# One fused transformer kernel on one core: the preparation of a state-space layer is spread over GpSimd and more buffers

## The chip, the cores and the metric

The kernel runs on 1 core of one Trainium2 chip. The metric is the device time of one execution in microseconds (us); the kernel before takes 1915.66 us, the median of 3 runs.

## The reference

The reference is two transformer blocks one after the other on 512 tokens of width 1024, in float32. The first has three branches (a chunked state-space scan, a gated linear recurrence and attention to a memory of 256 rows) that are gated, added and projected. The second has four layers, of which the first, a diagonal complex state-space layer called S5, matters here. Cut to its core:

```python
dt = jnp.exp(log_dt)[:, None]
ab = jnp.exp(lam * dt)                      # complex, (groups, states)
bb = (ab - 1) / lam * b                     # complex, (groups, states, 16)
bu = einsum('blgh,gph->blgp', u, bb)
s  = linear recurrence s_t = ab * s_(t-1) + bu_t
y  = gelu(real(einsum('blgp,ghp->blgh', s, c)) + d_skip * u)
out = (y * sigmoid(y @ w_glu + b_glu) * silu(z)) @ w_out
```

The memory attention, whose steps share the preparation's stretch of time, is softmax(q k^T / 16) v with 4 heads of 256 columns and 256 memory rows.

## The kernel before, in words

All wide matrix products are made of three float32r products each (high and low halves), so that TensorE is busy nearly all the time. A weight tile of 128x1024 is loaded by SP into one of 3 buffers, ScalarE rounds it to its high half (L317) and VectorE makes the low half (L318), into one of 7 pairs of buffers. Working tiles of 128x512 come from a pool of 36 (class Slots); it is a first-in, first-out list, and what is given back is handed out again in that order. A tile framework tracks the dependences, puts the instructions of each engine in an order before the run, by priority and a model of their durations, and adds the waits. SP issues the transfers in one queue; ScalarE and GpSimd have queues of their own.

**The preparation** (`s5_prep`, L1285) turns the parameters of S5 into tables in device memory: for each of 8 blocks b of 4 group pairs an input table W (winD), a response table E (eD) and a Toeplitz table T (toD). It has nothing to do with the tokens, and it is woven, by `yield`, into the last part of the linear recurrence and into the memory attention (`mem_`, L1152: 1.3 steps of the preparation for each step of the attention). Per block: L1380 to L1401 load the parameters and make bbr, bbi on VectorE; L1405 to L1413 make E with six VectorE operations (all through `tt`, L1288) and store it; L1418 to L1432 multiply on TensorE, put the result in Z, which is the first 256 columns of the buffer W0, and store it eight times, shifted, as T; L1434 to L1445 make W: for r = 0, 1 three VectorE operations of 128x512 write the factor into the one buffer f, four transposes (L1443) read it, ScalarE copies the result into W0 (L1444), and W0 is stored.

During one attention head (`mem_core`, L1092) the pool of 36 is held thus: 8 for `merged`, 4 keys, 4 values, 12 of the preparation (a8s, ps_, sc, PT 2, E0 2, W0 2, t, f, RT), prm and bbt, and the head's 2 queries: 32. Each of the four softmax rows of 128 tokens takes one buffer e from those left (L1116), and gives it back after its transposes (L1119) are issued.

**S5 itself** (`s5`, L1450): for each block m `inputs` multiplies u, sends it through device memory (uD, stored by ScalarE's queue at L1475, loaded by GpSimd's at L1478) to change its layout, and loads W. `starts` (L1486) makes chunk states, `scan` (L1500) runs the recurrence on VectorE in two halves, `within` (L1572) applies T, `outputs` (L1584) applies E to the states: ScalarE copies states (L1590), TensorE multiplies, VectorE adds (L1596), ScalarE applies gelu (L1598) and stores (L1599), GpSimd's queue loads the result in the other layout (L1602). `parts` (L1606) then splits y in halves for the next product (`split`: ScalarE at L471, VectorE at L472). `advance`, inside `scan`, takes two adjacent buffers for its products anew in each of its four calls. The loads of E (`fetch_e`, L1557) and T (`fetch_t`, L1545) go through SP's queue; E of blocks 0 to 3 goes to buffers that are free early.

Of the kernel before, what the change touches and what calls it, by code (L numbers as in the profile page):

```python
# [11 lines left out]
F32 = mybir.dt.float32  # L12
F32R = mybir.dt.float32r
I32 = mybir.dt.int32
AF = mybir.ActivationFunctionType
ALU = mybir.AluOpType
AX = mybir.AxisListType
PSUM = bass.MemoryType.PSUM
P = 128
# [188 lines left out]
class Kern:  # L208
# [258 lines left out]
    def split(self, hi, lo, src, scale=None):  # L467

        nc = self.nc
        if scale is None:  # L470
            nc.scalar.copy(hi, src)  # L471
            nc.vector.tensor_tensor(out=lo, in0=src, in1=hi.bitcast(F32), op=ALU.subtract)  # L472
        else:
            nc.scalar.activation(hi, src, AF.Copy if isinstance(scale, float) else AF.Identity, scale=scale)  # L474
            nc.vector.scalar_tensor_tensor(out=lo, in0=src, scalar=scale, in1=hi.bitcast(F32),  # L475
                                           op0=ALU.mult, op1=ALU.subtract)

    def wide(self):

# [805 lines left out]
    def s5_prep(self):  # L1285
        nc, S, I, p = self.nc, self.S, self.i, self.p
        V = nc.vector
        tt = lambda o, a, b, op: V.tensor_tensor(out=o, in0=a, in1=b, op=op)  # L1288
# [5 lines left out]
        ps_ = S.get()  # L1294
# [7 lines left out]
        sc = S.get()  # L1302
        w = [sc[:, 32 * j:32 * j + 32] for j in range(16)]
        PT, pts = S.run(2)
        PT = PT.rearrange("p a b -> p (a b)")[:, :576].rearrange("p (r j q) -> p r j q", r=2, j=9)
        E0, es = S.run(2)
        W0, ws = S.run(2)
        t, f = S.get(), S.get()
        RT = S.get()
        RT_ = RT.rearrange("p (r j q) -> p r j q", r=2, j=8)  # L1310
        dt, mag, th = w[0], w[1], w[2]
        self.exp_acc(dt, ld, w[8:12])
# [67 lines left out]
        for b in range(8):  # L1380
            qs = slice(4 * b, 4 * b + 4)
            prm = S.get()
            self.dma(out=prm[:, :256], in_=I["s5bc"][b])
            br, bi, cr, ci = [q4(prm[:, 64 * j:64 * j + 64]) for j in range(4)]
            nci = q4(prm[:, 256:320])
            V.tensor_scalar(nci, ci, -1.0, None, op0=ALU.mult)
            bbt = S.get()
            bbr, bbi, t1 = [q4(bbt[:, 64 * j:64 * j + 64]) for j in range(3)]
            f4 = lambda f: f[:, qs].unsqueeze(2).to_broadcast([P, 4, 16])
            tt(bbr, br, f4(fr), ALU.mult)  # L1390
            tt(t1, bi, f4(fi), ALU.mult)
            tt(bbr, bbr, t1, ALU.subtract)
            tt(bbi, bi, f4(fr), ALU.mult)
            tt(t1, br, f4(fi), ALU.mult)
            tt(bbi, bbi, t1, ALU.add)

            bd = bbt[:, 256:512].rearrange("p (r q z h) -> p r q z h", r=2, q=4, z=2)
            V.memset(bbt[:, 256:512], 0.0)
            for r, s in ((0, bbr), (1, bbi)):
                for z in range(2):  # L1400
                    V.tensor_copy(bd[64 * z:64 * z + 64, r, :, z], s[64 * z:64 * z + 64])  # L1401
            yield
            pw = lambda T, r, a: T[:, r, a:a + 8, qs].rearrange("p j q -> p q j").unsqueeze(3).to_broadcast([P, 4, 8, 16])
            x8 = lambda x: x.unsqueeze(2).to_broadcast([P, 4, 8, 16])
            E = E0.rearrange("p a b -> p (a b)").rearrange("p (q r n) -> p q r n", q=4, r=2)  # L1405
            ev = lambda r: E[:, :, r].rearrange("p q (j h) -> p q j h", j=8)
            tt(ev(0), pw(PT, 0, 1), x8(cr), ALU.mult)
            tt(q8(t), pw(PT, 1, 1), x8(ci), ALU.mult)
            tt(ev(0), ev(0), q8(t), ALU.subtract)
            tt(ev(1), pw(PT, 0, 1), x8(nci), ALU.mult)  # L1410
            tt(q8(t), pw(PT, 1, 1), x8(cr), ALU.mult)
            tt(ev(1), ev(1), q8(t), ALU.subtract)
            self.dma(out=self.eD[b], in_=E.rearrange("p q r n -> p (q r n)"))  # L1413
            yield

            g = self.tb()[:, 0:P]
            bl = lambda r, q: bd[:, r, q].rearrange("p z h -> p (z h)")
            self.in_order(True)  # L1418
            for r, c in ((0, cr), (1, nci)):
                for q in range(4):  # L1420
                    self.mm(g[32 * q:32 * q + 32, 0:16], bl(r, q), c[:, q], r == 0, r == 1)
            for r in range(2):
                for q in range(4):
                    self.mm(g[32 * q:32 * q + 32, 16:128], bl(r, q), E[:, q, r, 0:112], r == 0, r == 1)
            self.in_order(False)
            Z = W0.rearrange("p a b -> p (a b)")[:, 0:256]
            V.memset(Z[:, 0:128], 0.0)
            V.scalar_tensor_tensor(out=g[:, 0:16], in0=eye, scalar=dsk[:, b:b + 1], in1=g[:, 0:16], op0=ALU.mult, op1=ALU.add)
            nc.scalar.copy(Z[:, 128:256], g)
            dst = self.toD[b].rearrange("(t r q n) -> t q r n", t=8, r=32, q=4)  # L1430
            for k in range(8):
                self.dma(out=dst[k], in_=Z[:, 128 - 16 * k:256 - 16 * k])  # L1432
            yield
            W = W0.rearrange("p a b -> p (a b)").rearrange("p (q r n) -> p q r n", q=4, r=2)  # L1434
            for r in range(2):
                u, v, op = ((bbr, bbi, ALU.subtract), (bbi, bbr, ALU.add))[r]
                tt(q8(f), pw(RT_, 0, 0), x8(u), ALU.mult)
                tt(q8(t), pw(RT_, 1, 0), x8(v), ALU.mult)
                tt(f, f, t, op)
                yield  # L1440
                o = self.tb().rearrange("p (q n) -> p q n", q=4)
                for q in range(4):
                    nc.tensor.transpose(o[:, q], f[:, q * P:(q + 1) * P], self.ident)  # L1443
                nc.scalar.copy(W[:, :, r], o)  # L1444
            self.dma(out=self.winD[b], in_=W.rearrange("p q r n -> p (q r n)"))  # L1445
            S.put(prm, bbt)
            yield
        S.put(ps_, sc, RT, t, f, *pts, *es, *ws)

    def s5(self):  # L1450
        nc, S, R, I = self.nc, self.S, self.R, self.i
# [6 lines left out]
        SA, sas = S.run(8)  # L1458
# [27 lines left out]
        def starts(ms):  # L1486

            for m in ms:
                W, ws = Ws[m]
                v = self.tb().rearrange("p (r q c) -> p r q c", r=2, q=4)  # L1490
                for q in range(4):
                    for r in range(2):
                        for z in range(2):
                            self.mm(v[64 * z:64 * z + 64, r, q], W[:, q, r, 64 * z:64 * z + 64], g8(us[m])[:, 2 * q + z],
                                    True, True)
                nc.scalar.copy(SA[:, :, 4 * m:4 * m + 4, 1:64], v[:, :, :, 0:63])
                S.put(*ws)
                yield

        def scan(n):  # L1500
# [2 lines left out]
            qs = slice(16 * n, 16 * n + 16)  # L1503
            X = SA[:, :, qs]
            V = nc.vector
            prs = S.get()
            pr = [prs[:, 64 * j:64 * j + 64].rearrange("p (c r q) -> p c r q", c=2, r=2) for j in range(2)]

            def advance(k, src, dst, m):

                tmp, ts_ = S.run(2)
                t = tmp.rearrange("p a b -> p (a b)")[:, :32 * m].rearrange("p (r q c) -> p r q c", r=2, q=16)
                for c in range(2):
                    V.tensor_tensor(out=t, in0=X[:, :, :, src], op=ALU.mult,
                                    in1=self.a8[:, k, c, :, qs].unsqueeze(3).to_broadcast([P, 2, 16, m]))
                    V.tensor_tensor(out=t[:, 0], in0=t[:, 0], in1=t[:, 1], op=ALU.add)

                    V.tensor_tensor(out=X[:, c, :, dst], in0=X[:, c, :, dst], in1=t[:, 0], op=ALU.add)
                    yield
                S.put(*ts_)  # L1520

            yield from advance(0, slice(0, 63, 2), slice(1, 64, 2), 32)
            yield from advance(1, slice(1, 62, 4), slice(3, 64, 4), 16)
# [7 lines left out]
            S.put(prs)  # L1531
            yield from advance(1, slice(3, 60, 4), slice(5, 62, 4), 15)
            yield from advance(0, slice(1, 62, 2), slice(2, 63, 2), 31)

        zs, ys = [], []
        yh, yl = [R.get(), R.get()], [R.get(), R.get()]

        def gates(n):
# [18 lines left out]
        def fetch_e(m):  # L1557


            r, a = (yh, yl)[m // 2 % 2][m < 4], 2 * (m % 2)  # L1560
            Es[m] = [r[:, a + j].bitcast(F32) for j in range(2)]
            for j in range(2):
                last.append(self.dma(out=Es[m][j], in_=self.eD[m][:, 512 * j:512 * j + 512]))

        def fetch(f, *ms):

# [17 lines left out]
        def outputs(ms):  # L1584
            for m in ms:
# [6 lines left out]
                for q in range(4):  # L1592
                    for r in range(2):
                        self.mm(o[:, q * P:(q + 1) * P], E[q // 2][:, q % 2, r], B[:, r, q].rearrange("p z c -> p (z c)"),
                                r == 0, r == 1)
                nc.vector.tensor_tensor(out=us[m], in0=us[m], in1=o, op=ALU.add)  # L1596
                t = S.get()
                nc.scalar.activation(t, us[m], AF.Gelu_apprx_tanh)  # L1598
                nc.scalar.dma_start(out=by_time(yD[m]), in_=t)  # L1599
                S.put(t, us[m])  # L1600
                y = S.get()
# [3 lines left out]

        def parts(ms):  # L1606
            for m in ms:
                self.split(yh[m // 4][:, m % 4], yl[m // 4][:, m % 4], ys[m])
            yield

        run(inputs(range(5), self.gemm_early(True)))
# [539 lines left out]
```

## Time and profile before

| | |
|---|---|
| median of 3 runs | 1915.66 us (1913.89 to 1918.42) |
| the profiled execution, its own time | 1913.85 us |
| its span, first to last instruction | 1911.8 us |
| granted TensorE clock, mean | 0.994 of full speed |
| TensorE busy | 1866.1 us, 98% of the span |
| VectorE busy | 1298.0 us, 68% |
| ScalarE busy | 893.4 us, 47% |
| GpSimd busy | 57.3 us, 3% |

The profile is that of one execution. An engine's busy time is the sum of the time in which it ran an instruction; the time before an instruction in which its engine stood idle is put down to what released it. TensorE's ends are modelled, so that its busy share says that work was queued, not that the array was full. The preparation runs from about 665 to 950 us of the span, S5 from about 1000 to 1140 us.

### The profile page before, as it was taken

The page shows a single profiled execution, that of the slowest core. Times are in us where ns is not written, and L with a number is a line of the kernel's source. Part 1 is how long each engine was busy: PE and PEld are TensorE (multiplying, and loading weights), DVE is VectorE, ACT ScalarE, POOL GpSimd, SP SyncE. Part 2 cuts the span into 40 slices and gives each one's busy share as a digit, 9 for nine tenths or more (in the row PEclk, how much of TensorE's full clock was granted, in tenths as well). Part 3 has the DMA queues.
Part 4 walks back from the last instruction along what each step waited for, and adds up shares of the span by engine and source line. Part 5 has one row for each costly group of instructions (what it writes and reads, how often), then busy time and mean ns, then how long its engine had stood idle before and what let it go on. Part 6 is the DMA issues. An engine that isn't in the chain of part 4 may idle for free. (4 is left out here: it accounts for less than half of the span.)

```text
span 1911.8 us, 26275 instructions
## 1 busy us (share of the span) xinstructions
PE 1866.1 (98%) x9843; PEld 1517.1 (79%) x9843; DVE 1298.0 (68%) x2579; ACT 893.4 (47%) x1666; POOL 57.3 (3%) x93
## 2 busy tenths in 40 slices
PE   8999999999999999999999999999999999999998
PEld 7788877888888788778778878888887677788887
DVE  7886777665467897675475955787664776758553
ACT  5655545363565644332343444465544555534231
POOL 0100000000000000000001010000000000000000
PEclk9999999999999999999999999999999999999999
DMA  5543323323233436434668544232323122333421
GB/s 184 152 138 111 105 85 105 120 67 113 82 114 100 124 121 227 137 116 127 198 219 276 183 143 130 70 116 78 101 100 99 53 64 67 99 122 110 133 77 44
DMA packets 99201, 229.90 MB, mean 120 GB/s; under 512 B 18081, under 2 KB 38977, under 8 KB 99074
## 3 DMA queue, kind: packets, MB, share of 16 engines
q1 hardware_dynamic: 86192, 216.85, 35.3%
q0 software_dynamic: 2544, 6.00, 1.2%
q10 hardware_dynamic: 10338, 5.38, 1.0%
q8 instruction: 77, 1.26, 0.3%
q14 instruction: 50, 0.41, 0.1%
HBM read 200.28 MB, written 26.35 MB: 119 GB/s over the span
## 5 line engine op out<-in xcount | busy, mean ns | idle before, releaser
L277 PE MATMUL g<-rt,wh 128*128 128x512 f32 (+1 forms) x3664 | 1100.9, 383 | 11.2 <-ACT rt L471 7.4
L277 PEld LDWEIGHTS g<-rt,wh 128*128 128x128 f32 x3664 | 671.4, 190 | 147.5 <-ACT rt L471 9.1
L277 PE MATMUL g<-rt,wl 128*128 128x512 f32 (+1 forms) x1816 | 682.6, 380 | 0.0
L317 ACT CAST wh<-wf 128x1024 fp32r<-128x1024 f32 (+2 forms) x300 | 300.8, 1011 | 466.7 <-PE g L277 343.4
L318 DVE TENSOR_TENSOR wl<-wf,wh 128x1024 fp32r<-128x1024 f32 (+2 forms) x300 | 350.2, 1174 | 246.0 <-ACT wh L317 234.0
L277 PEld LDWEIGHTS g<-rt,wl 128*128 128x128 f32 x1816 | 343.8, 189 | 62.7 <-issue 1.9
L277 PE MATMUL g<-wh,rt 128*128 128x512 f32 x992 | 310.6, 393 | 0.7 <-DVE rt L475 0.7
L277 PEld LDWEIGHTS g<-wh,rt 128*128 128x128 f32 x992 | 185.6, 189 | 40.3 <-DVE rt L475 1.0
L277 PE MATMUL g<-wl,rt 128*128 128x512 f32 x496 | 194.0, 391 | 0.0
L277 PEld LDWEIGHTS g<-wl,rt 128*128 128x128 f32 x496 | 93.5, 189 | 19.7 <-issue 0.3
L277 PE MATMUL t<-st 128*64 128x64 f32 (+8 forms) x746 | 76.6, 274 | 5.7 <-DMA st<-uD 2.0
L665 DVE SCALAR_TENSOR_TENSOR st<-g,pc,st 128x511 f32<-128x511 f32 (+2 forms) x108 | 79.8, 744 | 2.0 <-ACT st L662 1.3
L1288 DVE TENSOR_TENSOR st<-st 128x512 f32<-128x512 f32 (+4 forms) x180 | 76.5, 467 | 6.3 <-PE t L1443 5.1
L275 PE MATMUL t<-st 128*64 128x128 f32 (+4 forms) x788 | 72.1, 296 | 0.8 <-ACT st L708 0.8
L277 PEld LDWEIGHTS t<-st 128*64 128x64 f32 (+3 forms) x746 | 44.1, 141 | 30.2 <-issue 16.4
L275 PEld LDWEIGHTS t<-st 128*64 128x64 f32 (+1 forms) x788 | 54.1, 143 | 16.2 <-issue 10.5
L1224 DVE TENSOR_TENSOR st<-g,st 128x512 f32<-128x512 f32 x32 | 22.0, 689 | 61.2 <-ACT st L1223 61.2
L277 PE MATMUL g<-st 128*128 128x256 f32 (+2 forms) x192 | 56.5, 426 | 5.6 <-DVE st L1265 2.4
L474 ACT ACTIVATE rt<-st 128x512 fp32r<-128x512 f32 x52 | 35.5, 711 | 50.4 <-DVE st L1649 16.3
L1223 ACT ACTIVATE st<-g 128x512 f32<-128x512 f32 x32 | 19.1, 597 | 77.5 <-PE g L277 77.5
L769 ACT ACTIVATE st<-st 128x128 f32<-128x128 f32 x128 | 40.7, 392 | 24.0 <-POOL st L765 23.8
L475 DVE SCALAR_TENSOR_TENSOR rt<-st,rt 128x512 fp32r<-128x512 f32 x52 | 38.4, 760 | 18.1 <-ACT rt L474 16.2
(303 smaller groups left out, 1838.7 us busy)
## 6 DMA issues: line engine op xcount, KB each, us to landing
wf<-in_w_xbc SPq DMA_DIRECT2D x24, 512.0 KB
wf<-in_w_gt SPq DMA_DIRECT2D x24, 512.0 KB
wf<-in_w_z SPq DMA_DIRECT2D x16, 512.0 KB
wf<-in_w_bs SPq DMA_DIRECT2D x16, 512.0 KB
rt<-acsD SPq DMA_DIRECT2D x24, 256.0 KB
wf<-in_w_lx SPq DMA_DIRECT2D x12, 512.0 KB
wf<-in_w_lg SPq DMA_DIRECT2D x12, 512.0 KB
wf<-in_w_bl SPq DMA_DIRECT2D x16, 384.0 KB
```

What stands on the lines that cost most here:

```text
L275: r = self.nc.tensor.matmul(out=out, lhsT=lhsT, rhs=rhs, start=start, stop=stop)
L277: r = self.nc.tensor.matmul(out=out, lhsT=lhsT, rhs=rhs, start=start, stop=stop)
L317: a = nc.scalar.copy(wh, wf)
L318: b = nc.vector.tensor_tensor(out=wl, in0=wf, in1=wh.bitcast(F32), op=ALU.subtract)
L474: nc.scalar.activation(hi, src, AF.Copy if isinstance(scale, float) else AF.Identity, scale=scale)
L475: nc.vector.scalar_tensor_tensor(out=lo, in0=src, scalar=scale, in1=hi.bitcast(F32), op0=ALU.mult, op1=ALU.subtract)
L665: nc.vector.scalar_tensor_tensor(out=out[:, d:], in0=ps[:, :512 - d], scalar=pcs(f"{n}w{j}", t), in1=out[:, d:], op0=ALU.mult, op1=ALU.add)
L769: nc.scalar.activation(m[:, j * P:(j + 1) * P], m[:, j * P:(j + 1) * P], AF.Exp, bias=self.nacs[:, c, h:h + 1])
L1223: nc.scalar.activation(y[:, c], ps, AF.Square, scale=1.0 / 32, accum_out=ss[:, i, n:n + 1])
L1224: nc.vector.tensor_tensor(out=y[:, c], in0=ps, in1=pg[n], op=ALU.mult)
L1288: tt = lambda o, a, b, op: V.tensor_tensor(out=o, in0=a, in1=b, op=op)
```

## The change

The three VectorE operations per factor become GpSimd operations. They are issued for both r before E is made, into two buffers f[0], f[1], with a buffer tf of their own for the products. Z gets a buffer zs with two halves, used in turn. The pool gives three buffers more to the preparation (zs, f[1], tf). In S5 `scan` takes its two product buffers once and keeps them to its end; the loads of E of blocks 0 and 1 wait for ScalarE's copy in `starts(3)`, those of blocks 2 and 3 for that in `starts(5)` (`behind`: with a semaphore); and the two halves of each split of y are put in their engines' order behind the gelu and the sum of the newest output issued (`after`: order alone, no semaphore).

```diff
@@ split
-            nc.scalar.copy(hi, src)
-            nc.vector.tensor_tensor(out=lo, in0=src, in1=hi.bitcast(F32), op=ALU.subtract)
+            a = nc.scalar.copy(hi, src)
+            b = nc.vector.tensor_tensor(out=lo, in0=src, in1=hi.bitcast(F32), op=ALU.subtract)
...
+        return a, b
@@ s5_prep
-        RT = S.get()
+        RT, zs = S.get(), S.get()
+        f, tf = [f, S.get()], S.get()
...
+            for r, (u, v, op) in enumerate(((bbr, bbi, ALU.subtract), (bbi, bbr, ALU.add))):
+                nc.gpsimd.tensor_tensor(out=q8(f[r]), in0=pw(RT_, 0, 0), in1=x8(u), op=ALU.mult)
+                nc.gpsimd.tensor_tensor(out=q8(tf), in0=pw(RT_, 1, 0), in1=x8(v), op=ALU.mult)
+                nc.gpsimd.tensor_tensor(out=f[r], in0=f[r], in1=tf, op=op)
...
-            Z = W0.rearrange("p a b -> p (a b)")[:, 0:256]
+            Z = zs[:, 256 * (b % 2):256 * (b % 2) + 256]
...
             for r in range(2):
-                u, v, op = ((bbr, bbi, ALU.subtract), (bbi, bbr, ALU.add))[r]
-                tt(q8(f), pw(RT_, 0, 0), x8(u), ALU.mult)
-                tt(q8(t), pw(RT_, 1, 0), x8(v), ALU.mult)
-                tt(f, f, t, op)
-                yield
                 o = self.tb().rearrange("p (q n) -> p q n", q=4)
                 for q in range(4):
-                    nc.tensor.transpose(o[:, q], f[:, q * P:(q + 1) * P], self.ident)
+                    nc.tensor.transpose(o[:, q], f[r][:, q * P:(q + 1) * P], self.ident)
                 nc.scalar.copy(W[:, :, r], o)
+                yield
@@ s5
-                nc.scalar.copy(SA[:, :, 4 * m:4 * m + 4, 1:64], v[:, :, :, 0:63])
+                added.append(nc.scalar.copy(SA[:, :, 4 * m:4 * m + 4, 1:64], v[:, :, :, 0:63]))
...
+            tmp, ts_ = S.run(2)
             prs = S.get()
...
-                tmp, ts_ = S.run(2)
...
-                S.put(*ts_)
...
             yield from advance(0, slice(1, 62, 2), slice(2, 63, 2), 31)
+            S.put(*ts_)
...
                 last.append(self.dma(out=Es[m][j], in_=self.eD[m][:, 512 * j:512 * j + 512]))
+                if m < 4:
+                    self.behind(last[-1], added[3 + m // 2 * 2])
...
-                nc.vector.tensor_tensor(out=us[m], in0=us[m], in1=o, op=ALU.add)
+                summed = nc.vector.tensor_tensor(out=us[m], in0=us[m], in1=o, op=ALU.add)
...
-                nc.scalar.activation(t, us[m], AF.Gelu_apprx_tanh)
+                ends[:] = [nc.scalar.activation(t, us[m], AF.Gelu_apprx_tanh), summed]
...
-                self.split(yh[m // 4][:, m % 4], yl[m // 4][:, m % 4], ys[m])
+                ab = self.split(yh[m // 4][:, m % 4], yl[m // 4][:, m % 4], ys[m])
+                for a, b in zip(ab, ends):
+                    self.after(a, b)
```

## Rows read from the trace of the kernel before

**Rows 1.** The page, busy us (share of the span) and instructions of each engine

```profile
PE 1866.1 (98%) x9843; PEld 1517.1 (79%) x9843; DVE 1298.0 (68%) x2579; ACT 893.4 (47%) x1666; POOL 57.3 (3%) x93
```

**Rows 2.** TensorE's timeline, 700 to 1140: start, us, instruction, [idle before, releaser]

```profile
712.06 0.66 PE L1443 MATMUL t<-ident,st 128*128 128x128 f32 x4 [2.54 <-DVE st L1288]
...
946.48 2.04 PE L277 MATMUL t<-st 32*128 32x128 f32 x16 [1.39 <-ACT st L1444]
...
1036.24 1.15 PE L277 MATMUL t<-st 128*64 128x64 f32 x32 [1.99 <-DMA st<-uD]
...
1113.35 5.75 PE L277 MATMUL t<-st,rt 128*128 128x128 f32 x48 [1.72 <-ACT st L1590]
1137.08 1.52 PE L277 MATMUL g<-rt,wh 128*128 128x512 f32 x2 [2.54 <-ACT rt L471]
```

**Rows 3.** Windows behind two of these waits: length, PE, PEld, DVE, ACT, POOL busy, clock, DMA

```profile
713.30:716.90 3.60, 3.60 (x20) 3.60 (x19) 3.60 (x6) 1.32 (x2) 0.00 (x0) 0.53 0.33 84
...
1136.50:1143.40 6.90, 6.32 (x14) 4.72 (x15) 3.21 (x4) 3.26 (x4) 0.00 (x0) 0.51 0.17 49
```

**Rows 4.** VectorE's groups by form: x count | busy us, mean ns | idle before

```profile
L318 DVE TENSOR_TENSOR wl<-wf,wh 128x1024 fp32r<-128x1024 f32 x260 | 316.5, 1224 | 223.7 <-ACT wh L317 211.8 <-PE t L1443 6.6 <-PE g L277 4.7
L1288 DVE TENSOR_TENSOR st<-st 128x512 f32<-128x512 f32 x96 | 64.1, 685 | 5.7 <-PE t L1443 5.1
```

**Rows 5.** A window of the preparation's densest part, columns as in rows 3

```profile
685.00:735.00 50.00, 47.46 (x378) 42.57 (x377) 45.03 (x101) 19.64 (x34) 0.00 (x0) 0.97 0.46 154
```

**Rows 6.** GpSimd's line 765 (ns min/median/max), and a VectorE instruction that met it

```profile
L765 POOL TENSOR_SCALAR_AFFINE_SELECT st<-rt x24: 629/637/2138, 71.1 to 283.2; 128x512 f32<-128x512 f32 x24
...
296.69 1.65 DVE L318 TENSOR_TENSOR wl<-wf,wh 128x1024 fp32r<-128x1024 f32 x1
```

**Rows 7.** The waits of 640 to 960: total us, times, longest

```profile
ACT st L1444 <- DMA toD<-st: 14.3, 4, 5.8
```

**Rows 8.** SP's, ScalarE's and GpSimd's timelines, 1005 to 1058: transfers issued

```profile
1009.97 9.59 SPq L270 DMA_DIRECT2D rt<-eD  x8
...
1020.71 0.37 ACTq L1475 DMA_DIRECT2D uD<-st  x1
1035.68 0.37 ACTq L1475 DMA_DIRECT2D uD<-st  x1
...
1032.84 0.54 POOL L1478 DMA_DIRECT2D st<-uD  x1 [10.49 <-issue]
1040.67 0.54 POOL L1478 DMA_DIRECT2D st<-uD  x1 [1.51 <-DMA uD<-st]
```

**Rows 9.** VectorE's and ScalarE's timelines at the end of S5, 1086 to 1140

```profile
1100.36 1.05 DVE L1514 TENSOR_TENSOR st<-st 128x480 f32<-128x480 f32 x1 [2.42 <-ACT st L1264]
...
1123.45 0.69 DVE L1596 TENSOR_TENSOR st<-st,t 128x512 f32<-128x512 f32 x1
...
1126.22 0.62 ACT L471 CAST rt<-st 128x512 fp32r<-128x512 f32 x1 [3.93 <-DMA st<-yD]
1127.69 0.63 ACT L1598 ACTIVATE st<-st 128x512 f32<-128x512 f32 x1
1136.41 0.62 ACT L471 CAST rt<-st 128x512 fp32r<-128x512 f32 x1 [5.10 <-DMA st<-yD]
```

**Rows 10.** One attention head's softmax, timelines of ScalarE, VectorE and TensorE, 774 to 783

```profile
775.37 0.48 ACT L1088 ACTIVATE st<-g,tiny 128x256 f32<-128x256 f32 x1 [1.58 <-DVE tiny L1087]
...
777.77 0.19 ACT L1088 ACTIVATION_READ_ACCUMULATOR st<-g,tiny 128x1 f32 x1
...
778.65 0.15 DVE L1089 RECIPROCAL tiny<-tiny 128x1 f32<-128x1 f32 x1
778.84 0.35 DVE L1090 TENSOR_SCALAR st<-st,tiny 128x256 f32<-128x256 f32 x1
...
779.29 0.39 PE L1119 MATMUL t<-ident,st 128*128 128x128 f32 x2
```

More of the change, by code (lines that the diff above doesn't have):

```diff
@@ L470, in split @@
         if scale is None:
-            nc.scalar.copy(hi, src)
-            nc.vector.tensor_tensor(out=lo, in0=src, in1=hi.bitcast(F32), op=ALU.subtract)
-        else:
-            nc.scalar.activation(hi, src, AF.Copy if isinstance(scale, float) else AF.Identity, scale=scale)
-            nc.vector.scalar_tensor_tensor(out=lo, in0=src, scalar=scale, in1=hi.bitcast(F32),
-                                           op0=ALU.mult, op1=ALU.subtract)
+            a = nc.scalar.copy(hi, src)
+            b = nc.vector.tensor_tensor(out=lo, in0=src, in1=hi.bitcast(F32), op=ALU.subtract)
+        else:
+            a = nc.scalar.activation(hi, src, AF.Copy if isinstance(scale, float) else AF.Identity, scale=scale)
+            b = nc.vector.scalar_tensor_tensor(out=lo, in0=src, scalar=scale, in1=hi.bitcast(F32),
+                                               op0=ALU.mult, op1=ALU.subtract)
+        return a, b
     def wide(self):
@@ L1447, in s5_prep @@
             yield
-        S.put(ps_, sc, RT, t, f, *pts, *es, *ws)
+        S.put(ps_, sc, RT, zs, t, *f, tf, *pts, *es, *ws)
     def s5(self):
@@ L1533, in scan @@
             yield from advance(0, slice(1, 62, 2), slice(2, 63, 2), 31)
-        zs, ys = [], []
+            S.put(*ts_)
+        zs, ys, added, ends = [], [], [], []
         yh, yl = [R.get(), R.get()], [R.get(), R.get()]
```

## The prediction

> **What bounds the kernel now.** The page comes first: TensorE is busy for 98% of the span [rows 1], so an edit on another engine is worth only what TensorE waits for that engine, and the change can remove little more than waits. TensorE's timeline over the stretch that the diff touches is therefore the next view. It shows five idle times of over 1 us, each ended by something that the diff edits [rows 2]. At 712.06 TensorE waits 2.54 us for VectorE to rewrite the single buffer f; at 946.48, 1.39 us for a copy into W0; at 1036.24, 1.99 us for the load of u; at 1113.35, 1.72 us for the copy of the states; at 1137.08, 2.54 us for the split of y. The reader is to see that these are 10.2 us of 1911.8.
>
> The windows come third. Behind such a wait the granted clock falls to about half, the 1.2 GHz level: 0.53 over 3.6 us behind the first, 0.51 over 6.9 us behind the last [rows 3]; behind the second and third there is a like stretch of 3.5 us at 0.52, behind the fourth none. A stretch costs its length times the missing share, so 3.6 x 0.47 = 1.7 us for each of the first three, 6.9 x 0.49 = 3.4 us for the last. A wait thus costs nearly double its idle time.
>
> **The change part by part.** *The factors of W.* For eight blocks, six VectorE operations of 685 ns [rows 4] go: 48 x 0.685 = 32.9 us of VectorE. In the densest 50 us VectorE is busy for 45.0 [rows 5]; there two blocks are made, so 8.2 us leave. With two buffers f the second factor need not wait for the first one's transposes; the wait at 712 goes with its clock, 2.54 + 1.7 = 4.2 us. What comes is 48 GpSimd operations with two inputs of 512 columns, which no row shows. The nearest has one input of that size: 637 ns, up to 2138 where it met VectorE [rows 6]. I bound one by 0.64 and 2.14 us and take twice the first, 1.28, since two inputs are read: 61 us over some 250 us in which GpSimd has nothing else. A block needs 7.7 us of it, and even at 2.14 us an operation all 48 take 103 us, so I take nothing for GpSimd itself.
>
> What VectorE gets back is less sure. An L318 of 1.22 us [rows 4] took 1.65 beside GpSimd's L765 [rows 6], and L765 stretched by 1.5 us beside VectorE: the two hold each other up where both read SBUF. In the dense stretch 12 operations could hold VectorE for between nothing and 12 x 1.28 = 15.4 us, against 8.2 removed; between a gain of 8.2 and a loss of 7.2 I take nought, the place near the middle, which the 5 idle us there leave hidden.
>
> The Trainium skill, "SBUF — State Buffer", section "Who interferes with whom", says that a VectorE instruction with two SBUF inputs and a GpSimd instruction that reads SBUF exclude each other for a whole instruction; the two rows above agree with it. By it the loss of 7.2 us is the one to expect while VectorE is full, and the words "beside VectorE" would not hold there.
>
> *Z in its own buffer.* W0 now also holds Z, whose eight stores must land before the next copy of W: ScalarE waits 14.3 us for them in 4 waits, the longest 5.8 [rows 7], and that one is what TensorE meets at 946. With zs the copies wait only for the store of W one block earlier. I take 1.39 + 1.7 = 3.1 us. The eight stores and their issue on SP's queue are as before.
>
> *The E loads tied.* SP issues all eight loads of E for blocks 0 to 3, 2 MB, in 9.6 us from 1009.97, when u is on its way through memory. The store of u issued at 1020.71 was followed by its load at 1032.84, 12.1 us later; the one issued at 1035.68, without E beside it, by its load at 1040.67, 5.0 us later [rows 8]. With E behind `starts(3)` and `starts(5)`, TensorE at 1036 should find u there: 1.99 + 1.7 = 3.7 us. The added semaphores stand in SP's queue; behind them are the loads of w_az, of T and of w_glu, and ScalarE's weight rounding would wait for those. Since these loads are themselves held by buffers in use, I take nothing; the cost is between nothing and the 3.7 us given back.
>
> *scan's buffers kept, splits last.* VectorE starts the scan's third pass 2.42 us late, waiting for a ScalarE instruction, as its product buffers had just been in use [rows 9]; kept buffers have no such wait, and the copy that TensorE meets at 1113 follows the end of that scan. At the end VectorE finishes the last sum at 1124.1, but ScalarE runs its gelu only at 1127.69, behind a split at 1126.22 that had waited 3.93 us for y; the last y then comes at 1136.41 [rows 9]. With the splits behind the gelus, that store leaves some 3.5 us earlier, more than the 2.54 us of TensorE's last wait. The whole is 1.72 + 2.54 + 3.4 = 7.7 us. What is late next are the splits themselves, eight in a row now on ScalarE at about 0.6 us each; I take half, 3.8.
>
> *Three buffers fewer for the others.* During an attention head the pool has four free buffers beside the 32 held; it will have one. All four softmax rows then use the same e, and each exponential waits for the transposes of the row before. Now four rows overlap, from 775.37 to 779.68, 4.3 us. One row alone is 0.48 + 0.19 + 0.15 + 0.35 + 0.39 = 1.56 us [rows 10], with three handovers guessed at 0.1 each 1.9, so a head needs 7.6 us. TensorE has the next head's two projections, 48 products, to fill it: at 1866.1 / 9843 = 0.19 us for a mean instruction [rows 1], 9 us at least. That covers it with 1.4 us to spare. If the cover is gone the price is that of the second rival; between nothing and 22 us I take 5, a little over 1 us a head, nearer the lower end because the sum of rows lies there.
>
> **The sum.** Gains: 4.2 + 3.1 + 3.7 + 3.8 = 14.8; cost 5. Against the profiled execution, 1913.85 us (2.05 around its span), that is 1904.1. This execution lies 1.8 us below the median of the runs shown, so on the median's scale I forecast **1906**. All gains whole (18.7) and no cost make 1897.
>
> **The rivals.** *VectorE is not relieved.* In the dense stretch the locks take the full 7.2 us; the wait at 712 stays and grows. Halfway, 4.5 us of waiting and clock are added and 4.2 lost: 1906 + 8.7 = 1914.7. For it speaks VectorE's 45.0 busy us of 50 and the 1.65 us row; against it that weight halves are made up to seven tiles ahead.
>
> *Softmax through one buffer, slower.* Place: `mem_core`, four heads. If a row takes more than 9 / 4 = 2.25 us, TensorE runs dry. With one VectorE operation of 0.69 and one lock of 0.64 in each row's way it is 3.2 us, so a head needs 12.9 us against 9: 3.8 idle plus 1.7 clock, four times 22 us. Less 14.8 gained, plus the 1.8 us: 1913.85 + 7.2 + 1.8 = 1923. It ends slower from about 2.9 us a row. For it speaks that ScalarE and VectorE are in-order queues with weight work of 1 us pieces in them; against it that heads' projections are there to be put in between, as TensorE's order already does with the rows of now.
>
> *The waits only move.* The order on each engine is made from a model, and other buffers mean other orders; TensorE may meet the same lateness one instruction on, and the pool hands out other buffers for the rest of the kernel. Gains of a third (5) less the cost of 5: 1915.7, no change.
>
> **How the numbers follow.** The measurement tells some 0.2%, 3.8 us, from no change: faster is below 1911.8, slower above 1919.5. Chances: the forecast 0.55 (its own range 1897 to 1911), VectorE not relieved 0.12, one buffer 0.16, waits moved 0.17. Faster: 0.55, with 0.03 of the first and 0.04 of the last rival, 0.62. Slower: 0.14 of the second, 0.02 of the last and 0.01 of the first, 0.17. The rest, 0.21, is no change. The range leaves out most of the one-buffer rival at the top and a tail below the full gains: 1897 to 1919.
>
> **What would show it.** Right: no wait of over 1 us at `L1443`, at swa_prep's small products behind the last W copy, or for uD; ScalarE's waits for toD gone; E loads after 1037; the last gelu right behind its sum; no half-clock stretch at these places. The locks: `wl` operations well over 1.22 us and GpSimd operations near 2 us between 690 and 940. The one buffer: ScalarE's exponentials (`L1088`) waiting for TensorE's transposes (`L1119`), and TensorE idle before those. The forecast is wrong if TensorE's idle time between 760 and 860 grows by over 10 us, or if the five waits come back under other lines.

## The result, and the profile after

The changed kernel takes 1945.24 us, the median of 4 runs (1943.07 to 1947.57), beside 1915.95 for the kernel before: the ratio is 1.016 [1.0141, 1.0179]. It is slower by 1.6%, where 1906 us was forecast.

Where the time goes is seen by dating the same work in both traces. ScalarE rounds 300 weight tiles (L317), and the start times of the same number, counted from 0, can be subtracted:

| start of weight rounding no. | 110 | 130 | 140 | 150 | 170 | 190 | 290 |
|---|---|---|---|---|---|---|---|
| before, us | 642.8 | 747.9 | 772.1 | 867.1 | 1010.1 | 1157.3 | 1809.9 |
| after, against before | +0.5 | +5.8 | +12.0 | +32.9 | +31.2 | +33.8 | +34.0 |

All of the loss arises between 640 and 900 us, in the preparation and the memory attention beside it. From no. 150 to no. 190, where S5 lies, +0.9 us is added; behind S5 nothing changes. (That S5 could have made some of the loss good, and does not, comes out in runs 9 and 16.)

The page's first part after the change (busy us, share of the span, instructions; answers to [rows 1]):

```profile
PE 1875.4 (96%) x9843; PEld 1523.9 (78%) x9843; DVE 1308.5 (67%) x2531; ACT 893.8 (46%) x1666; POOL 122.9 (6%) x141
```

This line already points at the cause. VectorE has 48 instructions fewer, worth 32.9 us, and yet is busy 10.5 us *longer* than before: its other instructions were stretched by 43.4 us. GpSimd gained 65.6 us. Which instructions were stretched stands in the groups by form (x count | busy us, mean ns | idle before):

```profile
L318 DVE TENSOR_TENSOR wl<-wf,wh 128x1024 fp32r<-128x1024 f32 x260 | 320.4, 1238 | 234.2 <-ACT wh L317 228.0 <-PE g L277 4.7 <-PE t L277 1.1
L1289 DVE TENSOR_TENSOR st<-st 128x512 f32<-128x512 f32 x48 | 45.7, 970 | 0.9 <-DMA eD<-st 0.7
...
L1411 POOL TENSOR_TENSOR st<-st 128x512 f32<-128x512 f32 x16 | 23.9, 1495 | 0.8
L1410 POOL TENSOR_TENSOR st<-st 128x512 f32<-128x512 f32 x16 | 22.5, 1408 | 17.3 <-DVE st L1289 16.6
L1409 POOL TENSOR_TENSOR st<-st 128x512 f32<-128x512 f32 x16 | 20.4, 1280 | 243.3 <-DVE st L1289 118.6 <-PE t L1445 59.3 <-issue 45.4
...
L1403 DVE COPY st<-st 64x64 f32<-64x64 f32 x32 | 15.0, 468 | 0.3
```

The operations of E, 685 ns before [rows 4], average 970. A GpSimd operation averages 1280 to 1495, near the 1.28 us of the prediction. The small copies of L1403 average 468; in the run with VectorE alone (below) they take 187.

One such meeting, on VectorE's and then GpSimd's timeline (start, us, engine, instruction):

```profile
808.67 0.39 DVE L1403 COPY st<-st 64x64 f32<-64x64 f32 x2
809.09 0.83 DVE L1289 TENSOR_TENSOR st<-st 128x64 f32<-128x64 f32 x2
809.84 2.16 DVE L1403 COPY st<-st 64x64 f32<-64x64 f32 x2
812.03 5.59 DVE L1289 TENSOR_TENSOR st<-st 128x512 f32<-128x512 f32 x4
...
819.34 0.14 DVE L1088 TENSOR_SCALAR tiny<-tiny 128x1 f32<-128x1 f32 x1
```

```profile
809.46 1.43 POOL L1410 TENSOR_TENSOR st<-st 128x512 f32<-128x512 f32 x1 [0.79 <-DVE st L1289]
810.85 1.10 POOL L1409 TENSOR_TENSOR st<-st 128x512 f32<-128x512 f32 x1
811.91 1.27 POOL L1411 TENSOR_TENSOR st<-st 128x512 f32<-128x512 f32 x1
813.25 1.43 POOL L1410 TENSOR_TENSOR st<-st 128x512 f32<-128x512 f32 x1
814.76 1.59 POOL L1411 TENSOR_TENSOR st<-st 128x512 f32<-128x512 f32 x1
```

Two copies of 64 columns take 0.39 us in a gap between two GpSimd operations and 2.16 us beside GpSimd; four operations of E take 5.59 us in place of 2.7. Behind them in VectorE's queue stand a weight half and then the first row of a softmax, and that row is what reaches TensorE: ScalarE waits 8.64 us for it, and TensorE 6.78 us for ScalarE at 820.19. The waits at 722 and 725 are for operations of E, the one at 1094 lies in S5 and is for u (run 16):

```profile
819.57 0.47 ACT L1089 ACTIVATE st<-g,tiny 128x256 f32<-128x256 f32 x1 [8.64 <-DVE tiny L1088]
```

```profile
722.13 0.60 PE L277 MATMUL t<-st 128*32 128x112 f32 x8 [3.83 <-DVE st L1289]
...
725.68 0.60 PE L277 MATMUL t<-st 128*32 128x112 f32 x8 [2.94 <-DVE st L1289]
...
820.19 2.50 PE L277 MATMUL g<-rt,wh 128*128 128x512 f32 x5 [6.78 <-ACT st L1089]
...
1094.41 1.98 PE L277 MATMUL t<-st 128*64 128x64 f32 x32 [6.23 <-issue]
```

Of the five old waits [rows 2] four are gone, and these stand in their place; the fourth, for the copy of the states (L1590, now L1595), is there still, 2.5 us in place of 1.72. Beside the five, TensorE had a wait that the prediction passed over, 1.6 us for a softmax's exponential; the 6.78 us are a wait of that kind. Before, and then after the change (waiting line, waited for: us in total, times, longest):

```profile
PE g L277 <- ACT st L1088: 1.6, 1, 1.6
```

```profile
PE g L277 <- ACT st L1089: 8.7, 2, 6.8
...
PE t L277 <- ACT st L1595: 2.5, 1, 2.5
```

The windows sum it up, two after the change and then the longer one before it (length; busy of PE, PEld, DVE, ACT, POOL; clock; DMA share; GB/s):

```profile
685.00:735.00 50.00, 42.41 (x295) 37.09 (x294) 45.47 (x84) 15.11 (x31) 20.73 (x16) 0.90 0.37 124
700.00:900.00 200.00, 172.48 (x975) 133.92 (x974) 131.88 (x249) 64.44 (x117) 50.94 (x37) 0.93 0.40 134
```

```profile
700.00:900.00 200.00, 194.48 (x1143) 155.55 (x1142) 134.11 (x287) 71.94 (x125) 0.00 (x0) 0.99 0.47 156
```

In the dense 50 us VectorE is as full as before, 45.47 against 45.03 [rows 5], with 17 instructions fewer; TensorE has 42.41 against 47.46. From 700 to 900 us TensorE was busy for 194.48 us at a clock of 0.99 before: 22.0 us less now, and a clock lower by 0.06 costs 10 to 12 us more (over the 172 busy us or all 200), together 32 to 34, the +32.9 of the table. Between 760 and 860 us TensorE's idle time grew from 3.0 to 14.3 us (busy 97.02 and 85.71 of 100): one of the prediction's own signs that it is wrong.

### The profile page after: what moved, and what is told of

It reads as the page before. It is cut to its first block, busy times and chain, and to the rows that moved or that the text cites. A ratio compares the mean times of both kernels' runs of the same rounds, so it can differ in the third digit from the quotient of the medians.

```text
span 1945.8 us, 26297 instructions
## 1 busy us (share of the span) xinstructions
PE 1875.4 (96%) x9843; PEld 1523.9 (78%) x9843; DVE 1308.5 (67%) x2531; ACT 893.8 (46%) x1666; POOL 122.9 (6%) x141
## 5 line engine op out<-in xcount | busy, mean ns | idle before, releaser
L318 DVE TENSOR_TENSOR wl<-wf,wh 128x1024 fp32r<-128x1024 f32 (+2 forms) x300 | 354.1, 1186 | 256.6 <-ACT wh L317 250.3
L317 ACT CAST wh<-wf 128x1024 fp32r<-128x1024 f32 (+2 forms) x300 | 300.6, 1011 | 473.2 <-PE g L277 327.6
L277 PEld LDWEIGHTS t<-st 128*64 128x64 f32 (+3 forms) x746 | 45.3, 146 | 43.4 <-issue 23.8
L1289 DVE TENSOR_TENSOR st<-st 128x64 f32<-128x64 f32 (+4 forms) x132 | 64.2, 531 | 1.6 <-DMA eD<-st 0.7
```

The source lines that it names most:

```text
L277: r = self.nc.tensor.matmul(out=out, lhsT=lhsT, rhs=rhs, start=start, stop=stop)
L317: a = nc.scalar.copy(wh, wf)
L318: b = nc.vector.tensor_tensor(out=wl, in0=wf, in1=wh.bitcast(F32), op=ALU.subtract)
```

## The experiments

Two theories stood against each other at first. By the **buffer theory** the three buffers held push all four softmax rows onto one (in the change, exponentials waited 18.4 us in 11 waits for the transposes of the row before). By the **port theory** GpSimd and VectorE stop each other. A third was the new **places** of the work. Every ratio is against runs of the kernel before made beside it, whose medians lay between 1911 and 1916 us; ratios, not medians, are compared.

**1. VectorE makes the factors, all else as changed.**

```diff
-                nc.gpsimd.tensor_tensor(out=q8(f[r]), ...
+                nc.vector.tensor_tensor(out=q8(f[r]), ...
```
(and so the other two.)

> The changed kernel with the 48 operations on the factors given back to VectorE, in the same new buffers and at the same places. Theory A (the 29 us come from the buffers: three more held, so the memory attention's softmax has one buffer for all four rows of a head): GpSimd is not the cause, the time stays at 1936 to 1946 us, and the rows of a head still follow each other by 2 to 4 us. Theory B (the 29 us come from GpSimd and VectorE holding each other up on 512-column operations): the copies of 64 columns are back at 0.2 us and the time falls to 1915 to 1922 us. Theory C (placement: the factors of both halves asked for before the E operations, the memset of Z waiting for its transfers): VectorE has the six operations ahead of E, the time is between, 1925 to 1935 us.

Measured: 1926.4 us, 1.0059 [1.0043, 1.0076]. About two thirds of the loss goes with GpSimd; a third stays. The page's line, and then VectorE's groups by form:

```profile
PE 1869.3 (97%) x9843; PEld 1519.5 (79%) x9843; DVE 1299.5 (68%) x2579; ACT 893.9 (46%) x1666; POOL 58.0 (3%) x93
```

```profile
L1289 DVE TENSOR_TENSOR st<-st 128x512 f32<-128x512 f32 x48 | 32.1, 683 | 0.0
...
L1403 DVE COPY st<-st 64x64 f32<-64x64 f32 x32 | 6.0, 187 | 0.3
```

VectorE does 48 operations more than in the change in 9.0 us less.

**2. Three buffers held, nothing else** (on the kernel before).

```diff
         RT = S.get()
+        held = [S.get() for _ in range(3)]
...
```

> The kernel before with three 2 KB buffers of the pool held, unused, while the preparation runs; nothing else. Theory A: the softmax rows fall onto one buffer and the time rises by 20 us or more, to 1936 to 1946 us. Theory B: the softmax loses a few us at most, 1916 to 1922 us. Theory C: as B.

Measured: 1915.0 us, 1.0004 [0.9991, 1.0017]. The rows did fall onto one buffer, as ScalarE's timeline shows:

```profile
775.06 0.48 ACT L1088 ACTIVATE st<-g,tiny 128x256 f32<-128x256 f32 x1 [1.58 <-DVE tiny L1087]
778.04 0.47 ACT L1088 ACTIVATE st<-g,tiny 128x256 f32<-128x256 f32 x1 [2.41 <-PE t L1119]
779.79 0.47 ACT L1088 ACTIVATE st<-g,tiny 128x256 f32<-128x256 f32 x1 [1.19 <-PE t L1119]
781.54 0.48 ACT L1088 ACTIVATE st<-g,tiny 128x256 f32<-128x256 f32 x1 [1.19 <-PE t L1119]
```

A row takes 1.75 us from then on, and the head's projections cover it: weight rounding 150 is 4.9 us late, no. 190 only 1.3. The buffer theory falls.

**3. The S5 edits alone** (ties, kept temporary, last splits, on the kernel before; diff as in the change).

> The kernel before with the parts of the change that lie in the S5 stage alone: loads of E tied behind the state copies, the scan's temporary kept, the last splits of y behind the last sum and Gelu. Prediction's reasons: the wait ahead of the first state multiplication (3.7 us) and half of the stalls at the end of S5 (3.8 us) go, 1908 to 1912 us. Reading of the trace after the change: the stage as a whole loses 2 to 3 us there (a new wait of 6 us for the load of u against one of 4 us gone), 1916 to 1920 us.

Measured: 1914.89 us, 1.0005 [0.9996, 1.0014]. No change, between the two expectations. Its trace shows a trade: TensorE has no wait of over 1 us left for the split of y, but one of 4.83 us ahead of a multiplication of u (1.99 before) and one of 2.71 us for the copy of the states (1.72 before). Runs 9 to 17 tell why.

**4. The change with a softmax in two half buffers.**

```diff
+            e2 = S.get()
...
-                e = S.get()
-                self.softmax(e[:, :256], sc, 256)
+                e = e2[:, 256 * (i % 2):256 * (i % 2) + 256]
+                self.softmax(e, sc, 256)
...
```

> The changed kernel, with the four rows of a head's softmax going in turn through the two halves of one buffer in place of whole buffers (a row needs 256 of its 512 columns), so that no row waits for the row just before it to be transposed; GpSimd and all else as in the change. Theory A: most of the loss is gone, 1914 to 1924 us, and rows follow each other by 1 to 1.5 us. Theory B: little is won, 1936 to 1946 us, since VectorE is still held up. Theory C: 1930 to 1940 us.

Measured: 1944.23 us, 1.0154 [1.0136, 1.0172]. The two rows of a pair now follow each other by 0.47 us, and it helps nothing that can be told: the buffer theory falls a second time.

**5. GpSimd's work with no reader.** On the kernel of run 2, GpSimd makes the factors a second time; VectorE keeps all its work.

```diff
+            for r, (u, v, op) in enumerate(((bbr, bbi, ALU.subtract), (bbi, bbr, ALU.add))):
+                nc.gpsimd.tensor_tensor(out=q8(held[r]), in0=pw(RT_, 0, 0), in1=x8(u), op=ALU.mult)
+                nc.gpsimd.tensor_tensor(out=q8(held[2]), in0=pw(RT_, 1, 0), in1=x8(v), op=ALU.mult)
+                nc.gpsimd.tensor_tensor(out=held[r], in0=held[r], in1=held[2], op=op)
```

> The kernel before with three buffers held (alone 1915 us) and with GpSimd making the factors of W a second time, at the place where the change makes them, into the held buffers; nobody reads them and VectorE keeps all its work. Theory B (GpSimd's 512-column operations stop VectorE's, whoever needs the result): the loss of the change comes back whole, 1930 to 1950 us, the more as VectorE has the 48 operations too, and VectorE's 64-column copies take over 1 us beside GpSimd. Rival (the loss is a wait for factors that come late from the slower engine): nobody waits, so 1913 to 1919 us.

Measured: 1947.55 us, 1.0175 [1.015, 1.02], against 1.0004 without these 48 operations: 33 us for results that nobody uses. The page's line and TensorE's longest wait:

```profile
PE 1873.7 (96%) x9843; PEld 1520.4 (78%) x9843; DVE 1342.1 (69%) x2579; ACT 893.7 (46%) x1666; POOL 125.2 (6%) x141
```

```profile
728.91 1.11 PE L1448 MATMUL t<-ident,st 128*128 128x128 f32 x4 [18.28 <-DVE st L1288]
```

Against run 2 (1299.5 us, the same 2579 instructions) VectorE is busy 42.6 us longer, as in the change (43.4). The port theory stands, and late factors are not needed to explain the loss.

**6. Factors on VectorE at their old places**, buffers, Z and S5 as changed.

> The changed kernel with the factors on VectorE (1926 us where they stand as in the change, ahead of E) and at the places that they had before, each half ahead of its own transposes; buffers, Z and S5 as in the change. Theory (the 12 us that are left without GpSimd come from asking for both halves ahead of E, so that VectorE is a stretch of twelve operations behind): 1913 to 1918 us. Rival (they come from Z's buffer, the ties or the held buffers together): 1924 to 1928 us.

Measured: 1925.19 us, 1.0054 [1.0027, 1.008], as run 1: the place costs nothing. What is left of the loss without GpSimd lies in Z, buffers or S5.

**7. Z alone**, in spare columns of the buffer of the powers (`Z = PT[:, 576:832]`), on the kernel before.

> The kernel before with Z alone in its own place (spare columns of the buffer of the powers, no further buffer). Prediction's reason: ScalarE no longer waits 14.3 us for the eight stores of Z ahead of the copies into W, so the TensorE wait of 1.4 us at 946 and some of that at 712 go: 1909 to 1914 us. Rival (ScalarE's wait stood beside other work; the memset of Z now waits in VectorE's queue instead): 1913 to 1918 us.

Measured: 1915.49 us, 1.0011 [0.9994, 1.0028]. The wait at 946 is gone, but TensorE waits 3.2 us for an exponential (1.6 before) and 2.1 us for VectorE's copy behind a softmax: the waits only moved.

**8. GpSimd's operations in quarters** (the three of run 1's place in a loop over q, 128 columns each).

> The changed kernel with each of GpSimd's 48 operations of 512 columns cut into four of 128. If GpSimd and VectorE hold each other up for the length of an instruction, the copies of 64 columns wait some 0.4 us in place of 1.1 and the time falls to 1930 to 1938 us. If what counts is GpSimd's busy time, whatever its pieces, or if the pieces cost GpSimd more in all, it stays at 1943 us or rises.

Measured: 1939.34 us, 1.0126 [1.0098, 1.0154]. The copies of L1403 fall:

```profile
L1403 DVE COPY st<-st x32: 177/367/445, 689.5 to 885.6; 64x64 f32<-64x64 f32 x32
```

The longest (ns, min/median/max) is 445 in place of 1118, though GpSimd is busy for 167.2 us in place of 122.9. Shorter operations hurt less: their median is 0.42 to 0.46 us in place of 1.18 to 1.46, and the copies' longest wait falls with it. VectorE is busy 1293.2 us, stretched by 28.1 us in place of 43.4. The whole time lies just above the expected range, so most of the loss stays; the intervals of this run and the change overlap a little.

**9. The change without its S5 edits, and 10. the new buffers alone** (VectorE makes the factors at the old places, no S5 edits).

> The changed kernel with its three edits in the S5 stage undone (E's loads free, the scan's temporary taken where it was, the last splits of y in no order). They cost nothing by themselves (1915 us alone). Theory (they take from the stage the slack in which a late start is made good: with them 290 to 292 us pass from the 150th to the 190th weight cast, without them 285 to 287 us where the preparation came late): 1938 to 1942 us. Rival (they neither cost nor bring): 1943 to 1947 us.

> The kernel before with the new buffers alone: Z in its own, two for the factors and one for their temporary, three more held in all; VectorE makes the factors where it did, S5 as before. Theory (buffers lose some 5 to 8 us in the memory attention, which S5 makes good without its edits): 1914 to 1919 us, against 1925 us with the S5 edits. Rival (Z's buffer with its memsets and copies costs by itself): 1922 to 1926 us.

Measured: 1941.22 us, 1.0138 [1.0116, 1.016], and 1918.23 us, 1.0026 [1.0012, 1.0041]. Between the two only GpSimd and the factors' place differ: 0.0112, or 21 us. The buffers cost some 5 us. Against run 6 the S5 edits cost 5 us on these buffers (1.0054 to 1.0026, intervals that overlap).

**11. A version: Z in the spare columns and two buffers f, all on VectorE; 12. the same with the last splits ordered.**

> A try at a version better than both: the kernel before with Z in the spare columns of the powers (no buffer; alone 1915 us) and the two halves of the factors in two buffers (one more from the pool), so that VectorE's second half does not wait for the transposes of the first; VectorE does all as before. Reason: VectorE is 22.5 of 25 us busy when TensorE waits at 712, and a wait of it there is lost: 1908 to 1914 us. Rival (as with each part alone, what is won in the memory attention is lost in S5's start or the reverse): 1913 to 1918 us.

> The run above with the last splits of y put behind the last sum and Gelu, as in the change, without the tied loads and the kept temporary. If the ordering shortens the end of S5 by half its stalls as predicted, 3 to 4 us below the run above. Rival: the same within 2 us, since the three S5 edits together brought nothing alone.

Measured: 1913.06 us, 0.9994 [0.9982, 1.0006], and 1912.79 us, 0.9992 [0.9981, 1.0004]. No change that can be told.

**13. The change without the tie; 14. the new buffers with the tie alone.**

```diff
-                if m < 4:
-                    self.behind(last[-1], added[3 + m // 2 * 2])
```

> The changed kernel with the loads of E free again; the kept temporary and the ordered splits stay. Theory (the tie moves 2 MB of E onto the last stores and loads of u, so that the eighth u lands over 10 us after its store and TensorE waits 6 us for it): the wait falls to 2 to 3 us and the time to 1938 to 1942 us, as with all three edits undone (1941). Rival (the kept temporary or the splits cost it): 1943 to 1946 us.

> The kernel with the new buffers alone (1918 us) and the loads of E tied as in the change. Theory: 1922 to 1926 us, with a wait of TensorE of 5 to 7 us for the last u. Rival: 1916 to 1920 us.

Measured: 1949.73 us, 1.0189 [1.0153, 1.0225], and 1912.94 us, 1.0005 [0.9989, 1.0022]. My theory of the tie was wrong in both directions: taken away it brought nothing, put in it cost nothing and, if anything, gained (4 us against run 10, intervals that overlap).

**15. Half of GpSimd's operations** (the first factor on VectorE, at the same place).

> The changed kernel with the first half's factors (24 operations) on VectorE at the same place and the second half's on GpSimd. If GpSimd's part goes with its operations, half of the 18.5 us between all on VectorE (1926) and all on GpSimd (1945) is left: 1933 to 1938 us. If the loss is set by the first operation that comes at a bad moment, it is at 1942 us or more; if VectorE's relief counts, it is above the mean of the two.

Measured: 1938.82 us, 1.0143 [1.011, 1.0177]: five sixths of the way from run 1 (1.0059) to the change (1.016), with an interval from the midpoint to beyond the change. Whether the loss goes with the number of operations stays open.

**16. The change with the scan's temporary taken per pass; 17. the new buffers with it kept.**

```diff
-            tmp, ts_ = S.run(2)
...
             def advance(k, src, dst, m):
+                tmp, ts_ = S.run(2)
```

> The changed kernel with the scan's temporary taken for each pass as before; tie and ordered splits stay. Theory (two buffers held through the serial part of the scan make stores and loads of u wait for their turn, and the starts with them): 1937 to 1942 us. Rival (the ordered splits, or only the three together): 1943 to 1948 us.

> The kernel with the new buffers alone (1918 us) and the scan's temporary kept as in the change. Theory: 1922 to 1926 us, the TensorE wait ahead of the last starts over 5 us. Rival: 1914 to 1920 us.

Measured: 1935.11 us, 1.0095 [1.0077, 1.0112], and 1926.14 us, 1.0049 [1.003, 1.0068]. Taken away it brings 12 us (1.016 to 1.0095), put in it costs some 4 (1.0026 to 1.0049, intervals that overlap): the kept temporary is the bad edit in S5. TensorE's wait for the copy of the states goes with it: 2.5 to 2.7 us in the four runs that have it (the change and runs 3, 13 and 17), 0.4 us at most in runs 9, 10, 14 and 16. In run 16:

```profile
PE t L277 <- ACT st L1595: 0.6, 2, 0.3
```

The window in which TensorE waited 6.23 us, in the change and then in run 16:

```profile
1080.00:1100.00 20.00, 13.77 (x120) 12.32 (x119) 14.23 (x45) 3.42 (x6) 0.54 (x1) 0.75 0.60 172
```

```profile
1080.00:1100.00 20.00, 20.00 (x175) 17.66 (x174) 18.94 (x52) 5.14 (x9) 0.54 (x1) 1.00 0.63 181
```

The 6.2 idle us, and the half of the clock that is missing behind them (0.50 from 1094.4 to 1103, 4 us), are 10 of the 12 us that separate them. How the buffers may reach so far is seen on SP's and GpSimd's queues, in the change and in run 16:

```profile
1072.33 7.99 SPq L270 DMA_DIRECT2D st<-toD  x3
...
1089.22 0.54 POOL L1481 DMA_DIRECT2D st<-uD  x1 [10.41 <-DMA uD<-st]
```

```profile
1072.28 0.60 SPq L270 DMA_DIRECT2D st<-toD  x1
...
1084.83 0.54 POOL L1481 DMA_DIRECT2D st<-uD  x1 [6.16 <-DMA uD<-st]
```

The last u was stored at 1079.8 in both. In the change three loads of T were issued from 1072.3 to 1080.3, in run 16 one; the load of u followed its store 9.4 us later, in run 16 it followed 5.1 us later. That the pool handed the T loads other buffers, and that they held the store up, is read from these rows; it wasn't tried by itself.

**18. The parts that won or cost nothing, together:** run 12 with the tie.

> Z in the spare columns of the powers, two buffers for the factors, all on VectorE (1913 us so far), with E's loads tied and the last splits ordered. If the tie's 5 us on the buffers alone can be had here too: 1906 to 1910 us, below both kernels. Rival (S5's start only makes good what was late before it, and here little is): 1911 to 1916 us.

Measured: 1911.36 us in 12 runs, 0.9977 [0.9964, 0.999]. It is the only version whose interval lies below the kernel before, by 0.2%, at the edge of what can be told; the expected 1906 to 1910 was too much.

## Why the prediction was wrong

**GpSimd's operations.** Their length was right (1.28 us estimated, 1.28 to 1.50 measured), their price was not. The step that failed is "I take nought, the place near the middle". Two things in it were wrong. First, the lock was priced by VectorE's busy sum in the densest 50 us alone. There VectorE's nought even came out (45.47 against 45.03), though TensorE was busy 5 us less; over the whole program VectorE was stretched by 43.4 us for 32.9 given. Second, the price was capped at 7.2 us, as if lateness were a sum. It is a delay of whatever stands next on VectorE: E's operations held TensorE's small products at 722 and 725, and ScalarE stood idle for 8.64 us before a softmax's first row at 819, in a stretch (760 to 860) where VectorE is busy for only 51.49 of 100 us. The prediction's list of five waits left out TensorE's wait of 1.6 us for a softmax's exponential, and the lock has no price there in its sum. Run 1 puts the term at 19 us and run 5 at 33; runs 9 and 10 give 21. The rival "VectorE is not relieved" named the mechanism, at a chance of 0.12 and a price of 8.7 us.

The Trainium skill, "SBUF — State Buffer", section "Who interferes with whom", has VectorE instructions with two SBUF inputs and GpSimd instructions that read SBUF exclude each other for a whole instruction. The rows of E's operations, which have two inputs, agree: 970 ns on average beside GpSimd's whole operations, 803 beside quarters (run 8), 683 without GpSimd (run 1). The copies of L1403 have one input and were stretched as well, which this rule alone does not cover. The prediction quoted the rule and then did not follow it.

**The wait at 712 and its clock (4.2 us gained).** Two waits for VectorE, 3.83 and 2.94 us, took its place in the change. With the factors on VectorE and two buffers f (run 11) no wait for f is left, but three for weight rounding, 4.5 us in all, come instead; no gain can be told.

**Z (3.1).** ScalarE no longer waits for toD ahead of W [rows 7]. In the change VectorE does, and holds ScalarE in turn (engine, line, waited for: us in total, times, longest):

```profile
ACT st L1436 <- DVE t L1435: 19.4, 5, 9.6
...
DVE st L1434 <- DMA toD<-st: 9.6, 4, 3.1
```

L1434 is the memset of Z, which the stores of the same half, two blocks earlier, must leave first; L1435 is VectorE's sum on the block's product, which L1436 then copies into Z (3.6 us of waiting before). Run 7 shows the gain of Z alone as nothing: the wait went, the time did not. "The waits only move" is what happened here.

**Ties, splits and kept buffers (3.7 and 3.8).** The tie did what was forecast of it, and was hidden. Without the kept temporary, adding ties and splits takes the change from 1.0138 (run 9) to 1.0095 (run 16), 8 us against 7.5 predicted; from weight rounding 150 to 190 run 16 makes 12.6 us of its lateness good, run 9 6.8. TensorE's waits of over 1 us ahead of the multiplications of u, 2.13 and 2.41 us in run 9, are gone in run 16, and run 14, with the tie alone, has none either where run 10 has 1.18 and 2.01. On the version of run 11 ties and splits give some 3 us (run 18), and TensorE's wait for uD, 2.0 us in run 11, is gone. That the splits gave any of this is not shown: runs 9, 10 and 11 have no wait of over 1 us for the split of y though nothing orders it there, and run 12 gains nothing by the order. The term that failed is the kept buffers: "kept buffers have no such wait" counted them as a gain. They cost 4 to 12 us, and the wait at 1113 that they were to end grew from 1.72 to 2.53 us. That this ate up what the tie had won fits the waits and the 1.0005 of run 3.

**One softmax buffer (5 taken, 0 to 22).** The row of 1.9 us was measured at 1.75, the cover held, and 4.9 us were lost at weight rounding 150 (run 2), as taken; by no. 190, behind S5, 1.3 us were left. The second rival, the dearest in the prediction, was the wrong fear. Why S5 makes up lateness without the kept temporary and not with it was not tried further.

**The sum as measured**, by the ratios: buffers +5 (run 10), GpSimd +21 (to run 9), ties and splits -8 (to run 16), kept temporary +12 (to the change), together 31 us, which is 1.016. These are steps of one path, so that they must add up; added in another order a term can differ, as the kept temporary's 4 us on run 10 shows.

## What to carry to other kernels

Work moved from VectorE to GpSimd need not be off VectorE: here 32.9 us were moved and VectorE got busier. Compare VectorE's busy time before and after, less what was taken from it, before anything else. Price such a meeting as a delay of whatever stands next in the slower engine's queue, at every place where it can happen, not as a sum over the densest stretch. And where buffers come from one first-in, first-out pool, test an edit that holds a buffer longer by itself: it can cost more than it saves, and hide what the edits beside it gain.

## What the runs showed that I had not expected

Two copies of 64x64, 0.19 us each, took 2.16 us beside GpSimd operations of 1.43 and 1.10 us: for their length the smallest instructions suffer most. And 48 GpSimd operations of 65.6 us in all stretched VectorE by 43.4 us, two thirds of their own length.
